# Chain and second inverse interleaved with latent attention, stick projections moved among the chunk preparations, chain products in 128 columns

## The chip, the cores and the metric

The kernel runs on one core of a Trainium2 chip. The metric is device time in microseconds from start to end of one execution. Five engines work side by side, each through its own queue in order: TensorE (PE; PEld is its weight load), VectorE (DVE), ScalarE (ACT), GpSimd (POOL) and SyncE (SP), which here issues every DMA.

## The reference

Two layers follow each other on a residual stream of 1024 positions by 1024 columns, float32. Each layer projects x to 2912 columns, which feed three kinds of heads, and mixes their results back:

```python
def stick_block(qb, start):          # 4 heads of 64, strict past only
    z = qb @ k.T * 64 ** -0.5
    log_keep = where(past, log_sigmoid(-z), 0)
    log_later = reverse_cumsum(log_keep) - log_keep
    return where(past, exp(log_sigmoid(z) + log_later), 0) @ v

def mla(q, k):                       # 4 heads: 64 plain + 32 rotary columns, causal
    return softmax(where(causal, q @ k.T * 96 ** -0.5, -inf)) @ v

def rwkv_step(state, r, w, k, v, kk, a):   # 8 heads, state 64 x 64, one step per position
    sa = state @ (-kk)
    state = state * w + sa * (kk * a) + v * k
    return state, state @ r

x = layer_norm(ALPHA * x + concat(o_sb, o_mla, o_rwkv) @ w_o)
u_act, u_gate = split(x @ ffn_w_up)
x = layer_norm(ALPHA * x + (gelu(causal_conv3(u_act)) * u_gate) @ ffn_w_down)
```

The per-position recurrence is computed in chunks of 64 positions: inside a chunk a triangular system has to be inverted, and between chunks a state is carried.

## The kernel before, in words

Every product that needs float32 accuracy splits its operands into a high and a low part and runs three matmuls (`mm3`, L200 to 204). A projection (`proj_h`, L241) computes 128 output columns for 1024 positions as 2 halves x 8 k-tiles x 3 = 48 matmuls of 512 columns. Its weights come through `wload` (L229): one DMA, a high part on ACT, a low part on DVE or POOL.

A layer runs in this order (`run`, L1117, and `phase_a`, L1046):

1. Projections and preparation of the latent heads (`mla_prep`).
2. Four chunk preparations, one per pair of recurrent heads: project k, r and v, then `rw_prep` and twice `rw_stage1` (L601; half the positions each), which make the chunk matrices and send them to DRAM. After the second and the fourth, `rw_inv` (L687) is made: a generator that inverts the triangles of four heads, mostly on DVE (L701 to 743), then on PE, and writes the result to DRAM. The first is stepped among the third and fourth preparation.
3. The gate's projection (`sg`), then the first chain (`rw_chain(0)`, L781) for heads 0 to 3, eight steps j of two chunks each, with the second inverse stepped three at a time between its steps.
4. The second chain, one step after each of the six stick projections (`proj_sb`, L260: two each of q, k and v; v is also transposed).
5. Attention: two streams of latent attention (`mla`, one per head of a pair) and two of stick attention (`stick`), 16 blocks of 128 queries each, in an order that `STREAM_ORDER` and `MLA_AHEAD` set.
6. Output projection, layer norm and feed-forward.

In a chain step, `rw_chain_q` (L799) loads four things from DRAM, multiplies them (L820) and brings the results to the tile QC (L821 to 823). `rw_chain_s` (L827) then does two state updates one after the other, each four products of 64 columns (L839) and two scalings on DVE (L842), and then the readout of eight products (L847). Such a float32 product is two instructions in the trace, so a step has 16 of them for its two updates and 16 for its readout. `rw_chain_y1` and `rw_chain_y2` normalise, add and gate.

A latent block takes scores on PE, a maximum on DVE (L541), an exponential on ACT (L546), a scaling on DVE (L559, L561), transposes (L327), and the product with v (L312). A stick block takes scores (L376, L377), a tanh on ACT (L378), a masking select on POOL (L384), and on DVE a scale (L385), a running product from the right (L387) and a combination (L388), then transposes and the product with v. A stick stream starts each head pair with copies and low-half splits of q and k (L350 to L361): on DVE for the first pair, on POOL in four pieces for the second.

The order on every engine is fixed when the program is built: a planner takes each engine's ready instructions by their place in the program, moved by the offsets in `PRIORITY` (weight loads and chain loads early, layer norms late). What a tile's buffers allow limits it. Of PSUM's eight banks, preparation and chains use pa 2, py 1, pq 1, mm 3, pi 1 (pi for the inverse); attention uses pa 2, py 1, pq 1, sc 2, av 2. The tag "pst" has four buffers that projections, attention loads and weights share.

Of the kernel before, what the change touches and what calls it, by code (L numbers as in the profile page):

```python
# [10 lines left out]
F32R = mybir.dt.float32r  # L11
# [30 lines left out]
MLA_AHEAD = 4  # L42
STREAM_ORDER = (-3, 0, 0, 1)
# [26 lines left out]
class Body:  # L70
# [38 lines left out]
    def constants(self):  # L109
# [23 lines left out]
        self.onesr = self.t(cp, [P, P], "onesr", F32R)  # L133
        nc.vector.tensor_copy(self.onesr, self.ones.to_broadcast([P, P]))
# [6 lines left out]
        self.m01 = self.t(cp, [P, W2], "m01")  # L141
        nc.vector.memset(self.m01, 1.0)
        nc.vector.memset(self.m01.rearrange("p (c i) -> p c i", i=C)[:, :, 0:1], 0.0)
# [116 lines left out]
    def proj_sb(self, l, pool, step):  # L260
        nc, W = self.nc, self.a["w_in"][l]
        for j in range(2):
            for base, dst in ((SBQ, self.sqd), (SBK, self.skd)):
                hi, lo = self.wload(W, [(base + j * P, P)], nc.gpsimd)
                d = self.t(pool, [P, S], "pst", bufs=4)
                self.proj_copy(hi, lo, d)
                nc.sync.dma_start(dst[j], d)
                step(4)
        for j in range(2):
            hi, lo = self.wload(W, [(SBV + j * P, P)], nc.gpsimd)  # L270
            d = self.t(pool, [P, S], "pst", bufs=4)
            self.proj_copy(hi, lo, d)
            o = self.t(pool, [P, S], "pst", bufs=4)
            for q in range(2):
                pt = self.ps2()
                for i in range(4):
                    ii = 4 * q + i
                    nc.tensor.transpose(pt[:, i * P : i * P + P], d[:, ii * P : ii * P + P], self.ident)
                nc.vector.tensor_copy(o[:, q * 512 : q * 512 + 512], pt)
            step(4)  # L280
            nc.sync.dma_start(self.svd[j], o.rearrange("p (i v) -> p i v", v=P))
# [38 lines left out]
    @prioritized  # L320
    def w_transpose(self, wt, w, nb, tag="av"):
# [59 lines left out]
    def stick_post(self, be, kp, i, LL, nb, n, V, hp, pr, wp):  # L381
        nc = self.nc
        dg = be[:, i * P : LL]
        nc.gpsimd.affine_select(out=dg, in_=dg, pattern=[[-1, P]], base=0, channel_multiplier=1, compare_op=ALU.is_gt, fill=-1.0)  # L384
        nc.vector.tensor_scalar(kp[:, : LL - 1], be[:, 1:LL], -0.5, 0.5, op0=ALU.mult, op1=ALU.add)  # L385
        kv = kp[:, : LL - 1][:, ::-1]
        nc.vector.tensor_tensor_scan(kv, kv, self.ones.to_broadcast([P, LL - 1]), 1.0, op0=ALU.mult, op1=ALU.mult)  # L387
        nc.vector.scalar_tensor_tensor(be[:, :LL], be[:, :LL], 1.0, kp[:, :LL], op0=ALU.add, op1=ALU.mult)  # L388
        wt = self.w_transpose(self.wt4[:, n % 6], be, nb, "pa")
        self.av_store(wt, nb, V, hp, self.mixd[pr], i, wp, "pa", 0.5)  # L390
# [20 lines left out]
    def mla_prep(self, l, mc, kp, wp):  # L411
        nc, a = self.nc, self.a
        ip = self.ip
        wr = self.t(kp, [P, 1280], "wr")
# [21 lines left out]
        def rms(js, n, gcol):  # L436
# [6 lines left out]
            for s in halves:  # L443
                ps = self.ps2()
                for j, (q, rows) in enumerate(sqs):
                    self.exact2(ps, self.onesr[:rows, :], q[:rows, s], wp, slice(0, rows))(j == 0, j == len(sqs) - 1)
                nc.scalar.activation(r[:, s], ps, AF.Ln, scale=1.0 / n, bias=self.rmse)
# [101 lines left out]
    def mla_post(self, st, e, pcs, n, nb, sc, pr, hp, i, V, wp):  # L549
# [12 lines left out]
        self.sn += 1  # L562
        wt = self.w_transpose(self.wt4[:, self.sn % 6], e, nb)
# [207 lines left out]
    def rw_chain_state(self, kp):  # L771
        nc = self.nc
        self.S_ = []
        for b in range(4):
            s_ = self.t(kp, [P, 2, 2, C], f"S{b}")
            nc.gpsimd.memset(s_, 0.0)
            nc.gpsimd.tensor_copy(s_[64:128, :, 0, :], self.ident[64:128, None, 64:128].to_broadcast([64, 2, 64]))
            nc.gpsimd.tensor_copy(s_[0:64, :, 1, :], self.ident[0:64, None, 0:64].to_broadcast([64, 2, 64]))
            self.S_.append(s_)

    def rw_chain(self, st, g2, tp):  # L781
        nc = self.nc
        for h in range(2):
            nc.gpsimd.memset(self.S_[0][h * 64 : h * 64 + 64, :, h, :], 0.0)
# [14 lines left out]
    def rw_chain_q(self, st, j, tp):  # L799
# [11 lines left out]
        QC = self.t(tp, [P, 2, 2, 2, P], "QC", bufs=2)  # L811
        PSh = PS.rearrange("p (f h) e x -> p f h e x", h=2)
        RBh = RB.rearrange("p (f h) c x -> p f h c x", h=2)
        for h in range(2):
            kr = slice(h * 64, h * 64 + 64)
            dr = slice(64 - h * 64, 128 - h * 64)
            pQ = self.pst("pa").rearrange("p (f e x) -> p f e x", f=2, e=2)
            for f in range(2):
                for e in range(2):
                    nc.tensor.matmul(pQ[:, f, e, :], PSh[:, f, h, e, :], RBh[:, f, h, e, :], start=True, stop=True)  # L820
# [6 lines left out]
    def rw_chain_s(self, st, j, QC):  # L827
        nc = self.nc
        fs = slice(2 * st, 2 * st + 2)
        ps = self.pst(("py", "pq")[j % 2])  # L830
        pY = ps[:, 0:256].rearrange("p (f h v) -> p f h v", f=2, h=2)
        pSS = ps[:, 256:512].rearrange("p (e f v) -> p e f v", e=2, f=2)
        for e in range(2):
            c_ = 2 * j + e
            Sc, Sn = self.S_[c_ % 4], self.S_[(c_ + 1) % 4]
            pS = pSS[:, e]
            for f in range(2):
                for h in range(2):
                    nc.tensor.matmul(pS[h * 64 : h * 64 + 64, f, :], QC[:, f, h, 1 - e, C:P], Sc[:, f, h, :], start=True, stop=True)  # L839
            for h in range(2):  # L840
                kr = slice(h * 64, h * 64 + 64)
                nc.vector.tensor_tensor(Sn[kr, :, h, :], pS[kr], self.Gc[kr, c_, fs, None].to_broadcast([64, 2, 64]), op=ALU.mult)  # L842
        for e in range(2):
            Sc = self.S_[(2 * j + e) % 4]
            for f in range(2):
                for h in range(2):
                    nc.tensor.matmul(pY[e * 64 : e * 64 + 64, f, h, :], QC[:, f, h, 1 - e, 0:C], Sc[:, f, h, :], start=True, stop=True)  # L847
        return pY

    def rw_chain_y1(self, pY, tp):  # L850
# [3 lines left out]
        py4 = pY.rearrange("p f h v -> p (f h) v")  # L854
        ys = self.t(tp, [P, 4, C], "ys", bufs=Y_LAG + 1)
        nc.scalar.copy(ys, py4)
# [189 lines left out]
    def phase_a(self, l, side, other, lp, co, cc):  # L1046
# [20 lines left out]
        self.split(*w2a2, raw)  # L1067
        self.Vz = []
# [12 lines left out]
        for ft in range(4):  # L1081
# [22 lines left out]
        ch = self.rw_chain(0, g2, tp)  # L1104
        for _ in ch:
            step(3)
        step(99)
        ch = self.rw_chain(1, g2, tp)

        def cstep(n):  # L1110
            next(ch, None)

        self.proj_sb(l, pp, cstep)
        for _ in ch:
            pass

    def run(self):  # L1117
# [28 lines left out]
        for l in range(L):  # L1146
# [6 lines left out]
            self.psum(cp, pa=(512, 2), py=(512, 1), pq=(512, 1))  # L1153
            with ExitStack() as c:
                self.psum(c, mm=(512, 3))
                self.psum(c, pi=(512, 1))
                cc = ExitStack()
                self.phase_a(l, side, other, lp, co, cc)
# [3 lines left out]
            with ExitStack() as c:  # L1162
                self.psum(c, sc=(512, 2), av=(512, 2))
                aw = self.pool(c, "attn", bufs=2, side=side)
                ms = [self.mla(aw, hp) for hp in range(2)]
                self.wt4 = self.t(self.ip, [P, 6, NT, P], "Aa")
                self.kp3 = [self.t(self.ip, [P, S], n) for n in ("LA", "T", "pd")]
                for t in self.kp3:
                    nc.gpsimd.memset(t, 0.0)
                for _ in range(MLA_AHEAD):  # L1170
                    next(ms[0])
                cc.close()
                self.w0h = self.t(self.wq, [P, 2, D], "w0h", F32R)
                self.w0l = self.t(self.wq, [P, 2, D], "w0l", F32R)
                aw3 = self.pool(c, "attn3", bufs=2, side=other)
                st = [self.stick(aw3, self.ip, hp) for hp in range(2)]
                seq = sorted([(t + o, n, g) for n, (g, o) in enumerate(zip((ms[0], st[0], ms[1], st[1]), STREAM_ORDER)) for t in range(17)], key=lambda x: x[:2])
                for _, _, g in seq:
                    next(g, None)
# [49 lines left out]
```

## Time and profile before

| what | value |
|---|---|
| time, median of 3 runs | 3151.99 us (3151.85 to 3153.93) |
| the profiled execution | 3154.05 us, span 3152.3 us |
| PE busy | 2993.2 us (95%) |
| DVE busy | 1796.4 us (57%) |
| ACT busy | 1058.6 us (34%) |
| POOL busy | 330.7 us (10%) |
| mean granted TensorE clock | 0.981 of full speed |

An engine is busy from an instruction's start to its end; matmuls are pipelined, so PE's busy time counts overlapping ones once and says little of how full it is. The chain that ended last is PE for 26% of the span, by 18% in three lines of `mm3`. A clock of 1.0 is 2.4 GHz, 0.5 is 1.2 GHz, and a mean in between is a mix of the two. Layer 1's mixer is at 128 to 746 us of the span, layer 2's at 1690 to 2305.

### The profile page before, as it was taken

What the parts mean: (1) busy time and instruction counts of PE and PEld (TensorE: products, weight loads), DVE (VectorE), ACT (ScalarE), POOL (GpSimd) and SP (SyncE); (2) the same over time, 40 slices, a digit from 0 to 9 for tenths busy, and PEclk for the clock granted to TensorE, in tenths of its full rate; (3) what the DMA queues carried; (4) which work ended last, traced back from release to release, by engine and by line L of the source; (5) the groups of instructions that cost most, each with busy time, mean ns of one, the idle gap of its engine ahead of it and who ended that gap; (6) DMA issues with size and microseconds to landing.
All of it is one profiled execution on the core that took longest, in us unless ns stands there. A gap on an engine that the chain in (4) does not pass through costs nothing. (4 is left out here: it accounts for less than half of the span.)

```text
span 3152.3 us, 42021 instructions
## 1 busy us (share of the span) xinstructions
PE 2993.2 (95%) x16572; PEld 2421.2 (77%) x16572; DVE 1796.4 (57%) x2842; ACT 1058.6 (34%) x1865; POOL 330.7 (10%) x346
## 2 busy tenths in 40 slices
PE   8998999988999999999999989999789999999998
PEld 6677777776888888888877767777678888888887
DVE  4587764876644444444746877567865444344436
ACT  5444343764122112222144443446532211122220
POOL 0112131132000000000001111311310000000000
PEclk9999899999999999999999999999899999999999
DMA  4344566323421111111234456662235111111111
GB/s 129 97 141 110 169 186 191 97 62 121 149 85 50 51 41 47 54 50 51 64 84 127 108 132 193 178 190 53 81 121 172 54 47 40 43 56 49 54 47 54
DMA packets 339284, 301.79 MB, mean 96 GB/s; under 512 B 25224, under 2 KB 304016, under 8 KB 339088
## 3 DMA queue, kind: packets, MB, share of 16 engines
q1 hardware_dynamic: 339088, 299.11, 32.1%
q8 instruction: 131, 2.15, 0.3%
q14 instruction: 65, 0.53, 0.1%
HBM read 208.87 MB, written 90.18 MB: 95 GB/s over the span
## 5 line engine op out<-in xcount | busy, mean ns | idle before, releaser
L202 PE MATMUL psmm<-xTh,whi 128*128 128x512 f32 x2144 | 852.9, 398 | 0.0
L204 PE MATMUL psmm<-xTh,wlo 128*128 128x512 f32 x2144 | 852.1, 397 | 0.0
L203 PE MATMUL psmm<-xTl,whi 128*128 128x512 f32 x2144 | 852.1, 397 | 0.0
L197 ACT CAST whi<-raw 128x1024 fp32r<-128x1024 f32 x152 | 159.9, 1052 | 1111.3 <-PE psmm L203 1076.1
L204 PEld LDWEIGHTS psmm<-xTh,wlo 128*128 128x128 f32 x2144 | 405.2, 189 | 93.2 <-issue 4.3
L202 PEld LDWEIGHTS psmm<-xTh,whi 128*128 128x128 f32 x2144 | 405.4, 189 | 92.9 <-issue 4.4
L203 PEld LDWEIGHTS psmm<-xTl,whi 128*128 128x128 f32 x2144 | 405.3, 189 | 92.8 <-issue 3.9
L198 DVE TENSOR_TENSOR wlo<-raw,whi 128x1024 fp32r<-128x1024 f32 x122 | 148.8, 1220 | 424.5 <-ACT whi L197 424.5
L1031 DVE TENSOR_TENSOR y<-y,psps 128x512 f32<-128x512 f32 x288 | 196.2, 686 | 171.8 <-PE psps L204 171.4
L202 PE MATMUL psps<-wdh,hh 128*128 128x512 f32 x672 | 266.8, 397 | 0.0
L203 PE MATMUL psps<-wdl,hh 128*128 128x512 f32 x672 | 263.1, 391 | 0.0
L204 PE MATMUL psps<-wdh,hl 128*128 128x512 f32 x672 | 260.1, 391 | 0.0
L894 POOL TENSOR_TENSOR lrs<-lrs,mhalf 128x1 f32<-128x1 f32 x32 | 29.1, 910 | 1637.7 <-DVE lrs L893 1637.7
L202 PEld LDWEIGHTS psps<-wdh,hh 128*128 128x128 f32 x672 | 126.1, 188 | 36.4 <-ACT hh L197 5.5
L204 PEld LDWEIGHTS psps<-wdh,hl 128*128 128x128 f32 x672 | 126.2, 188 | 27.0
L203 PEld LDWEIGHTS psps<-wdl,hh 128*128 128x128 f32 x672 | 126.3, 188 | 25.8
L1006 DVE TENSOR_TENSOR cv<-cv,psmm 128x1024 f32<-128x1024 f32 x44 | 53.7, 1221 | 143.3 <-PE psmm L204 138.4
L198 DVE TENSOR_TENSOR wdl<-raw,wdh 128x1024 fp32r<-128x1024 f32 x42 | 51.4, 1225 | 88.5 <-ACT wdh L197 88.5
L198 POOL TENSOR_TENSOR wlo<-raw,whi 128x1024 fp32r<-128x1024 f32 x30 | 76.0, 2532 | 242.5 <-ACT whi L197 242.4
L312 PE MATMUL pspa<-Aa,mv 128*128 128x128 f32 x576 | 86.4, 298 | 4.4 <-ACT Aa L328 3.8
L312 PEld LDWEIGHTS pspa<-Aa,mv 128*128 128x128 f32 x576 | 77.1, 207 | 17.5 <-ACT Aa L328 15.8
L820 PE MATMUL pspa<-RBl,PSl 128*128 128x128 f32 x512 | 73.4, 292 | 17.2 <-ACT QC L823 11.8
(443 smaller groups left out, 4777.4 us busy)
## 6 DMA issues: line engine op xcount, KB each, us to landing
raw<-in_ffn_w_up_dram SPq DMA_DIRECT2D x88, 512.0 KB
raw<-in_w_in_dram SPq DMA_DIRECT2D x44, 512.0 KB
raw<-in_ffn_w_down_dram SPq DMA_DIRECT2D x44, 512.0 KB
rbd<-RB SPq DMA_DIRECT2D x64, 256.0 KB
PSl<-psd SPq DMA_DIRECT2D x32, 512.0 KB
RBl<-rbd SPq DMA_DIRECT2D x32, 512.0 KB
psd<-Vz SPq DMA_DIRECT2D x64, 128.0 KB
xxd<-X SPq DMA_DIRECT2D x64, 128.0 KB
```

The costliest lines, as they stand in the source:

```text
L197: self.nc.scalar.copy(hi, src)
L198: (eng or self.nc.vector).tensor_tensor(lo, src, hi.bitcast(F32), op=ALU.subtract)
L202: mm(out, lh, rh, start=start, stop=False)
L203: mm(out, lh, rl, start=False, stop=False)
L204: mm(out, ll, rh, start=False, stop=stop)
L312: self.nc.tensor.matmul(av, V[:, j, :], wt[:, j, :], start=j == 0, stop=j == nb - 1)
L820: nc.tensor.matmul(pQ[:, f, e, :], PSh[:, f, h, e, :], RBh[:, f, h, e, :], start=True, stop=True)
L894: nc.gpsimd.tensor_tensor(rs, rs, self.mhalf[:, 0:1], op=ALU.pow)
L1006: nc.vector.tensor_tensor(cv, cv, pg, op=ALU.mult)
L1031: nc.vector.tensor_tensor(y[:, i, hs], y[:, i, hs], ps, op=ALU.add)
```

## The change

`proj_sb` becomes one projection per call and is called twice after each of the first three chunk preparations; the transposed v copies go from DVE to ACT. `phase_a` ends with the gate's projection and hands the second inverse and both chains, not yet run, to a new `phase_b`. There, for 19 turns, a chain step, three steps of the inverse, a block of the first latent stream and (three turns later) one of the second follow each other; the inverse is finished at turn 7, before the second chain begins, and the chains at turn 15. Stick attention follows alone, its two streams one turn apart. The bank pi stays through this, av has one buffer, and latent attention's transposes alternate between pi and av.

QC is laid out anew, so that one product takes both heads of a pair (for the states) or both chunks of a step (for the readout) in 128 columns; half of each result, the cross terms, is not used. `maskA`'s neighbours `onesr` and `m01` are made once a layer instead of once.

```diff
-    def proj_sb(self, l, pool, step):
+    def proj_sb(self, l, pool, n):
...
-                nc.vector.tensor_copy(o[:, q * 512 : q * 512 + 512], pt)
+            nc.scalar.copy(o[:, q * 512 : q * 512 + 512], pt)
...
-            pt = self.pst(tag)
+            pt = self.pst(tags[(j0 // 4 + 1) % len(tags)])
...
-        wt = self.w_transpose(self.wt4[:, self.sn % 6], e, nb)
+        wt = self.w_transpose(self.t(wp, [P, NT, P], "mwt", bufs=2), e, nb, ("av", "pi"))
...
-            nc.vector.tensor_tensor(QC[kr, :, h, :, 0:C], pQ[kr, :, :, 0:C], arl[kr], op=ALU.add)
-            nc.vector.tensor_tensor(QC[kr, :, h, :, C:P], pQ[kr, :, :, C:P], self.ident[kr, None, None, h * 64 : h * 64 + 64].to_broadcast([64, 2, 2, 64]), op=ALU.add)
-            nc.scalar.copy(QC[dr, :, h], pQ[dr])
+            nc.vector.tensor_tensor(QY[kr, :, h], pQ[kr, :, :, 0:C], arl[kr, :, ::-1, :], op=ALU.add)
+            nc.vector.tensor_tensor(QS[kr, :, :, h], pQ[kr, :, :, C:P], self.ident[kr, None, None, h * 64 : h * 64 + 64].to_broadcast([64, 2, 2, 64]), op=ALU.add)
+            nc.scalar.copy(QS[dr, :, :, h], pQ[dr, :, :, C:P])
+            nc.scalar.copy(QY[dr, :, h], pQ[dr, :, :, 0:C])
...
             for f in range(2):
-                for h in range(2):
-                    nc.tensor.matmul(pS[h * 64 : h * 64 + 64, f, :], QC[:, f, h, 1 - e, C:P], Sc[:, f, h, :], start=True, stop=True)
+                nc.tensor.matmul(pS[:, e, f], QC[:, 1, f, e], Sc[:, f], start=True, stop=True)
...
-                    nc.tensor.matmul(pY[e * 64 : e * 64 + 64, f, h, :], QC[:, f, h, 1 - e, 0:C], Sc[:, f, h, :], start=True, stop=True)
+                nc.tensor.matmul(pY[:, f, h], QC[:, 0, f, h], self.S_[j % 2][:, :, f, h, :], start=True, stop=True)
...
+            if ft < 3:
+                for n in range(2 * ft, 2 * ft + 2):
+                    self.proj_sb(l, pp, n)
...
+        return inv, [self.rw_chain(st, g2, tp) for st in range(2)]
+
+    def phase_b(self, l, side, other, c, cc, inv, chains):
+        nc = self.nc
+        aw = self.pool(c, "attn", bufs=2, side=side)
+        ms = [self.mla(aw, hp) for hp in range(2)]
+        for t in range(19):
+            if t < 16:
+                next(chains[t // 8], None)
+            if t == 15:
+                for ch in chains:
+                    for _ in ch:
+                        pass
+            for _ in range(3):
+                next(inv, None)
+            if t == 7:
+                for _ in inv:
+                    pass
+            if t < 16:
+                next(ms[0])
+            if t >= 3:
+                next(ms[1])
...
+        cc.close()
...
+        st = [self.stick(aw3, self.ip, hp) for hp in range(2)]
+        for t in range(18):
+            for n in range(2):
+                if t >= n:
+                    next(st[n], None)
```

## Rows read from the trace of the kernel before

**Rows 1.** The page, parts 1 and 2: busy time by engine, and by slice.
```profile
PE 2993.2 (95%) x16572; PEld 2421.2 (77%) x16572; DVE 1796.4 (57%) x2842; ACT 1058.6 (34%) x1865; POOL 330.7 (10%) x346
...
PE   8998999988999999999999989999789999999998
```
**Rows 2.** Busy time by stage: stretch, length, engines (instructions), clock, DMA share.
```profile
128.00:364.00 236.00, 213.94 (x1516) 169.06 (x1514) 173.25 (x296) 111.45 (x213) 49.29 (x50) 0.94 0.46 127
364.00:475.00 111.00, 101.92 (x946) 82.74 (x946) 81.56 (x156) 41.49 (x78) 29.23 (x24) 0.95 0.61 188
475.00:553.00 78.00, 74.18 (x559) 58.22 (x557) 34.65 (x94) 26.38 (x51) 14.70 (x15) 1.00 0.62 189
553.00:746.00 193.00, 169.83 (x1165) 145.78 (x1165) 153.10 (x309) 127.92 (x346) 44.17 (x55) 0.96 0.27 74
...
sum 615.00, PE 546.22 PEld 449.00 DVE 444.64 ACT 305.90 POOL 135.15; mean PE 136.56 PEld 112.25 DVE 111.16 ACT 76.48 POOL 33.79
```
**Rows 3.** PE's longest waits, 128 to 364 us: total, times, longest.
```profile
PE pspq L655 <- DVE q L632: 4.2, 1, 4.2
PE pspq L576 <- DVE q L198: 4.1, 1, 4.1
```
**Rows 4.** Stretches of the third preparation, columns as in rows 2.
```profile
223.00:238.00 15.00, 8.91 (x36) 6.41 (x34) 14.41 (x34) 6.47 (x11) 2.59 (x2) 0.87 0.14 37
...
257.00:270.00 13.00, 8.77 (x37) 7.12 (x37) 13.00 (x18) 4.69 (x11) 3.03 (x1) 0.80 0.16 42
```
**Rows 5.** PE in order of time, inside a projection: start, length.
```profile
180.32 0.39 PE L202 MATMUL psmm<-xTh,whi 128*128 128x512 f32 x1
180.55 0.40 PE L203 MATMUL psmm<-xTl,whi 128*128 128x512 f32 x1
```
**Rows 6.** DVE by line, 364 to 553 us: chain's and inverse's first and last.
```profile
L821 DVE TENSOR_TENSOR QC<-pspa,arl 64x256 f32<-64x256 f32 x32 | 13.5, 422 | 25.6 <-PE pspa L820 23.2 <-PE pspq L847 1.1 <-PE pspy L847 0.6
L705 DVE TENSOR_TENSOR pd<-LA,T 128x2 f32<-128x2 f32 (+18 forms) x19 | 13.5, 710 | 0.6
...
L859 DVE TENSOR_SCALAR vs<-vs 128x4 f32<-128x4 f32 x14 | 3.0, 213 | 0.2
...
L726 DVE STREAM_TRANSPOSE LA<-T 128x1024 f32<-128x1024 f32 x1 | 2.2, 2200 | 0.0
```
**Rows 7.** DVE by line, 553 to 746 us: latent's and sticks' first and last.
```profile
L541 DVE TENSOR_REDUCE mst<-pssc 128x1 f32<-128x512 f32 (+3 forms) x48 | 26.1, 548 | 7.6 <-PE pssc L204 5.4 <-PE pssc L539 2.1
L387 DVE TENSOR_TENSOR_SCAN pd<-pd,ones 128x255 f32<-128x255 f32 (+5 forms) x11 | 15.1, 1374 | 0.1
...
L361 DVE TENSOR_TENSOR kl<-pst,kh 96x1024 fp32r<-96x1024 f32 (+1 forms) x5 | 6.1, 1212 | 0.0
...
L385 DVE TENSOR_SCALAR T<-mexp 128x383 f32<-128x383 f32 (+5 forms) x11 | 5.0, 456 | 2.1 <-POOL mexp L384 2.0
...
L552 DVE RECIPROCAL mst<-mst 128x1 f32<-128x1 f32 x16 | 2.4, 153 | 4.2 <-ACT mexp L546 4.2
```
**Rows 8.** Stretches of chain with inverse, and of attention; columns as in rows 2.
```profile
364.00:440.00 76.00, 69.08 (x609) 55.15 (x608) 65.86 (x128) 26.83 (x49) 20.27 (x13) 0.96 0.64 201
...
553.00:640.00 87.00, 79.36 (x566) 67.72 (x567) 71.62 (x178) 63.52 (x182) 8.58 (x17) 1.00 0.32 86
```
**Rows 9.** POOL by line, 553 to 746 us: the sticks' splits.
```profile
L361 POOL TENSOR_TENSOR qh<-pst,qh 64x256 fp32r<-64x256 f32 x8 | 12.9, 1642 | 1.0 <-ACT qh L350 1.0
...
L361 POOL TENSOR_TENSOR kl<-pst,kh 128x256 fp32r<-128x256 f32 x8 | 8.6, 1098 | 4.6 <-ACT kh L351 4.6
```
**Rows 10.** PE in order of time, inside the first chain: start, length.
```profile
412.61 0.40 PE L847 MATMUL pspy<-S,QC 128*64 128x64 f32 x4
...
414.95 0.45 PE L839 MATMUL pspq<-S,QC 128*64 128x64 f32 x8
...
415.83 0.39 PE L876 MATMUL pspa<-sg,g 128*128 128x128 f32 x2
```
**Rows 11.** ACT by line, 364 to 553 us.
```profile
L823 ACT COPY QC<-pspa 64x512 f32<-64x512 f32 x32 | 18.6, 581 | 31.3 <-DVE QC L822 24.0 <-issue 6.0 <-PE pspa L820 0.9
```

More of the change, by code (lines that the diff above doesn't have):

```diff
@@ L258, in proj_T @@
         return pt
-    def proj_sb(self, l, pool, step):
+    def proj_sb(self, l, pool, n):
         nc, W = self.nc, self.a["w_in"][l]
[L262 to L278, printed above, removed]
-                nc.vector.tensor_copy(o[:, q * 512 : q * 512 + 512], pt)
-            step(4)
-            nc.sync.dma_start(self.svd[j], o.rearrange("p (i v) -> p i v", v=P))
+        j = n % 2
+        base, dst = ((SBQ, self.sqd), (SBK, self.skd), (SBV, self.svd))[n // 2]
+        hi, lo = self.wload(W, [(base + j * P, P)], nc.gpsimd)
+        d = self.t(pool, [P, S], "pst", bufs=4)
+        self.proj_copy(hi, lo, d)
+        if n < 4:
+            nc.sync.dma_start(dst[j], d)
+            return
+        o = self.t(pool, [P, S], "pst", bufs=4)
+        for q in range(2):
+            pt = self.ps2()
+            for i in range(4):
+                ii = 4 * q + i
+                nc.tensor.transpose(pt[:, i * P : i * P + P], d[:, ii * P : ii * P + P], self.ident)
+            nc.scalar.copy(o[:, q * 512 : q * 512 + 512], pt)
+        nc.sync.dma_start(dst[j], o.rearrange("p (i v) -> p i v", v=P))
     def proj_mla(self, l, pool):
@@ L413, in mla_prep @@
         ip = self.ip
+        onesr = self.t(kp, [P, P], "onesr", F32R)
+        nc.vector.tensor_copy(onesr, self.ones.to_broadcast([P, P]))
         wr = self.t(kp, [P, 1280], "wr")
@@ L445, in rms @@
                 for j, (q, rows) in enumerate(sqs):
-                    self.exact2(ps, self.onesr[:rows, :], q[:rows, s], wp, slice(0, rows))(j == 0, j == len(sqs) - 1)
+                    self.exact2(ps, onesr[:rows, :], q[:rows, s], wp, slice(0, rows))(j == 0, j == len(sqs) - 1)
                 nc.scalar.activation(r[:, s], ps, AF.Ln, scale=1.0 / n, bias=self.rmse)
@@ L853, in rw_chain_y1 @@
         vs = self.t(tp, [P, 4], "vs", bufs=Y_LAG + 1)
-        py4 = pY.rearrange("p f h v -> p (f h) v")
+        py4 = pY.rearrange("p f h e v -> p (f h) e v")
         ys = self.t(tp, [P, 4, C], "ys", bufs=Y_LAG + 1)
-        nc.scalar.copy(ys, py4)
+        for e in range(2):
+            er = slice(64 * e, 64 * e + 64)
+            nc.scalar.copy(ys[er], py4[er, :, e])
         nc.scalar.activation(yq, ys, AF.Square)
@@ L1067, in phase_a @@
         self.split(*w2a2, raw)
+        self.m01 = self.t(tp, [P, W2], "m01")
+        nc.gpsimd.memset(self.m01, 1.0)
+        nc.gpsimd.memset(self.m01.rearrange("p (c i) -> p c i", i=C)[:, :, 0:1], 0.0)
         self.Vz = []
@@ L1103, in phase_a @@
         self.rw_chain_state(kp)
[L1104 to L1115, printed above, removed]
+        return inv, [self.rw_chain(st, g2, tp) for st in range(2)]
[19 more added lines that the diff above has]
+                next(ms[1])
+        for m in ms:
+            next(m, None)
+        self.wt4 = self.t(self.ip, [P, 6, NT, P], "Aa")
+        self.kp3 = [self.t(self.ip, [P, S], n) for n in ("LA", "T", "pd")]
+        for t in self.kp3:
+            nc.gpsimd.memset(t, 0.0)
+        cc.close()
+        self.w0h = self.t(self.wq, [P, 2, D], "w0h", F32R)
+        self.w0l = self.t(self.wq, [P, 2, D], "w0l", F32R)
+        aw3 = self.pool(c, "attn3", bufs=2, side=other)
+        st = [self.stick(aw3, self.ip, hp) for hp in range(2)]
[3 more added lines that the diff above has]
+                    next(st[n], None)
     def run(self):
@@ L1152, in run @@
             self.Gc = self.t(lp, [P, NCH, 4], "Gc")
-            self.psum(cp, pa=(512, 2), py=(512, 1), pq=(512, 1))
+            self.psum(cp, pa=(512, 2), py=(512, 1), pq=(512, 1), pi=(512, 1))
             with ExitStack() as c:
                 self.psum(c, mm=(512, 3))
-                self.psum(c, pi=(512, 1))
                 cc = ExitStack()
-                self.phase_a(l, side, other, lp, co, cc)
+                inv, chains = self.phase_a(l, side, other, lp, co, cc)
             cx.close()
@@ L1162, in run @@
             with ExitStack() as c:
[L1163 to L1179, printed above, removed]
+                self.psum(c, sc=(512, 2), av=(512, 1))
+                self.phase_b(l, side, other, c, cc, inv, chains)
                 nxt = self.mix_load(NT - 1)
```

43 lines of the change are left out of this document (16 added, 27 removed).

## The prediction

> **What bounds the kernel now.** I read the page first: TensorE (PE) is busy 95% of the span, so at most about 159 us could come from filling its holes, and the slices place them: full in the feed-forward stretches, 7 to 9 tenths in the mixer stretches [rows 1]. Then the stage table, which cuts layer 1's mixer at 128, 364, 475, 553 and 746 us: chunk preparation, first chain with second inverse, second chain with stick projections, attention [rows 2]. The reader is to see there that no engine binds all four. In preparation VectorE (DVE) is busy 173 us and PE 214 of 236; in the first chain 82 and 102 of 111; in the second chain DVE only 35 of 78, because six projections keep PE full; in attention 153 and 170 of 193. Layer 2's four stretches sum to 615 us against 618. A busy PE is not a full PE: back-to-back 512-column matmuls start every 0.23 us but each is drawn 0.39 us long [rows 5], so PE's figures are upper ends and DVE's can be summed. Third, who waits in preparation: PE waits for DVE, 4.2 and 4.1 us at the longest [rows 3], in two stretches where DVE is busy 96 to 100%, PE only 59 to 67%, and the granted clock falls to 0.87 and 0.80 of 2.4 GHz [rows 4]. The last view is the DVE groups by line, from which each stream's load is summed.
>
> **The change, part by part, for one layer.**
>
> *Projections into preparation.* Six projections of 48 matmuls leave the second chain: 288 x 0.23 = 66 us of PE [rows 5]; the same 66 us go into preparation. DVE gets nothing with them (the weights' low halves are split on POOL, busy 49 of 236 us there [rows 2]); the two transposed V copies move from DVE to ACT. What can come back is PE's waste in the 236 us: 236 - 213.9 = 22 us not busy, and a mean clock of 0.94, which means 12% of the time at 1.2 GHz, a loss of at most 0.06 x 236 = 14 us. So the refund lies between 0 and 36 us. I take half, 18 us: the two projections after the second preparation give the first inverse's DVE work 22 us more to run under, and that is where both long waits and the low clock stand [rows 3, 4]. The other half stays, since the short waits of PE on masks and squares happened although projections were already there as filler. Each projection needs one of four "pst" buffers, of which k, r and v hold three, so no more than about one runs ahead inside a preparation. Preparation: 236 + 66 - 18 = 284 us, so +48.
>
> *Chains, second inverse and latent attention together, sticks alone.* Before, 364 to 746 us is 382 us; without the 66 us of projections 316. After, DVE binds. Its load by stream: the chains' eight groups run from 13.5 down to 3.0 us and sum to 66.0, with 4.0 more after 553: 70 us. The inverse's seven groups, 13.5 to 2.2, sum to 48 us [rows 6]. Latent attention's eight groups, 26.1 to 2.4, sum to 64, and eight low-half splits of 1.21 us make 74. The sticks' nine scan, scale and product groups, 15.1 to 5.0, sum to 86, and their four splits make 91 [rows 7]. First pass (chains, inverse, latent attention) 70 + 48 + 74 = 192 us, second pass (sticks) 91 us; with sg's shift, 284. PE and ACT have slack: ACT was busy 41 + 26 + 128 = 196 of these 382 us [rows 2]. DVE's share of such a stretch is the whole question: 0.82 where four attention streams run (553 to 640), 0.87 where chain and inverse run with projections (364 to 440) [rows 8], 0.96 to 1.00 where inverse and preparation saturate it [rows 4]. I take 0.88, near the second, since the first pass keeps the inverse's DVE-only ladder as filler for its first half: 284 / 0.88 = 322 us, +6 against 316. Of it the sticks take about 106 (91 plus some 15 for the small blocks and the change of head pair). The ends: 0.96 gives 296 (-20), attention's whole 153.1/193 = 0.79 gives 359 (+43).
>
> *Products in 128 columns.* Eight state-product instructions of 64 columns take 0.45 us with the last 0.22 us long, so seven starts in 0.23 us: two at a time. The readouts come singly, four in 0.40 us, 0.06 apart; a 128-column fp32 piece starts 0.11 after the one before [rows 10]. A chain step had 16 + 16 such pieces, 16/2 x 0.058 + 16 x 0.058 = 1.39 us, and gets 8 + 8 of 0.112 = 1.79: +0.4 x 16 steps = 6 to 7 us of PE. If every state round waits for its products it is also 32 x 0.22 = 7 us of path; I charge 0, since DVE and not PE binds the first pass, and keep 7 as the upper end.
> The Trainium skill, TensorE: Matmul & The Clock Gate, Part 3, says that matmuls with few output rows run at the same time when their outputs lie in different column groups. By that rule all 32 pieces would have gone in pairs, and the loss would be 0.86 x 16 = 14 us a layer; the rows show pairs for the state products alone, so 7 is the bound I keep.
>
> *Copies and single buffers.* QC leaves PSUM in 64 ACT copies of 256 elements instead of 32 of 512, which took 0.58 us [rows 11]; if each costs 0.29 (half) to 0.58 it is 0 to +19 us of ACT, under ACT's slack of half the stretch. A readout copy becomes two. Latent attention's transposes lose one PSUM buffer: behind a waiting transpose stand all of PE's later matmuls, and a copy of 0.58 exposed in each of 32 blocks would be 19 us; I charge 0 while DVE is behind, 19 at most. All DMAs go through SP's queue: the chains' 64 loads now stand among the attention's stores, and a store that waits for its block holds the next chunk's load; two chunks are in flight at some 14 us each, so 0, and if that cover fails one load's wait per chunk is in the 0.79 end. Memsets of m01 and onesr, once a layer: under 1 us, hidden.
>
> *Sum.* Per layer +48 for preparation, -66 + 6 = -60 for the rest: -12. Two layers: -24. The profiled execution took 3154.05 us (span 3152.3), 2.1 above the median 3151.99: 3130 in its terms, 3128 in the median's.
>
> **Rivals.**
>
> *The stick pass starves* (slower). Place: the 32 stick blocks. Today latent attention's reductions fill DVE while a stick block goes PE, ACT, POOL select, DVE; one of the sticks' three scale groups still idled 2.1 us for that select [rows 7]. Alone, two streams must cover it, and at the change of head pair POOL splits q and k for 12.9 + 8.6 = 22 us [rows 9], of which the two widest blocks in hand cover about 10 (86 us over 32 blocks is 2.7 us at a mean width of 576, so 4.8 at 1024). At a DVE share of 0.70 the pass is 91/0.70 + 12 = 142 instead of 106: +36 over the forecast, per layer -12 + 36 = +24, in all 3128 + 72 = 3200. It decides from a stick pass of about 118 us. Against it: three blocks are in flight, and two widest ones hold DVE for 9.6 us.
> The Trainium skill, Perfetto Trace Analysis, Optimization Strategy, advises interleaving regimes whose most contended engine differs. The second chain did that, with DVE busy 35 and PE 74 of 78 us [rows 2]; the change pairs DVE-heavy with DVE-heavy. It speaks for this side, by no figure of its own.
>
> *Everything fills* (faster by more). The whole 36 us comes back and DVE runs at 0.93 (305 us, -11): -47 a layer, 3058. For: DVE already reaches 0.96 and more where it has enough ready [rows 4]. Against: neither of the longer stretches reached 0.9 [rows 8].
>
> *No change.* The planner already used projections as filler, so moved ones only displace others: refund 6, rest +6, 3152.
>
> **How the numbers follow.** Forecast 0.38, stick starvation 0.32, everything fills 0.15, no change 0.15. About 0.2% (6 us) is what a measurement of this kernel can tell from no change. The forecast's own spread is a DVE share of 0.86 to 0.91 (330 to 312) with the refund fixed: 3108 to 3144. Faster: 0.34 + 0.15 + 0.03 = 0.52; same: 0.03 + 0.09 = 0.12; slower: 0.32 + 0.01 + 0.03 = 0.36. The range goes down to 3065, which leaves out half of "everything fills", and up to 3210, which leaves out about a third of the starvation cases: together a little under 2 in 10.
>
> **What would show it.** Preparation from the first mask multiply to the last should take about 284 us a layer, with PE's waits on DVE during the first inverse gone and the clock there at 1.0; if it takes 300, the refund failed. From there to the output projection some 322 us, DVE at 0.88 or above; the stick scans (L387 before) should lie in their own stretch of about 106 us, and a stretch of 118 or more with DVE waiting for POOL's select and splits is the rival. The chain products should be half as many, 0.11 us apart, and no wait of DVE on them should grow past 7 us a layer. Wrong altogether if layer 1's mixer is longer than 618 us.

## The result, and the profile after

The changed kernel took 3285.77 us (median of 4 runs, 3275.36 to 3290.04) beside 3152.96 us of the kernel before: 1.0416 times as long, interval 1.0389 to 1.0442, so 133 us slower. The forecast was 3128 us, in a range of 3065 to 3210. The profiled execution took 3288.49 us, span 3286.8.

The page after, parts 1 and 2, answering to [rows 1]:

```profile
PE 3050.8 (93%) x16060; PEld 2470.1 (75%) x16060; DVE 1794.7 (55%) x2833; ACT 1081.9 (33%) x1969; POOL 343.3 (10%) x346
...
PE   8998988967999999999999989789679999999998
```

DVE's work is the same to 2 us, and the feed-forward slices are as full as before. What is new are emptier slices in the two mixers. The stage table says where (stretch, length, busy time of PE, PEld, DVE, ACT and POOL with their instructions, granted clock, DMA share, GB/s); layer 1 in five stretches (preparation; first chain with the inverse; the joint between the chains; second chain; sticks alone), layer 2's three below (preparation; chains with latent attention; sticks), and last the preparation of layer 2 in the kernel before:

```profile
128.00:437.00 309.00, 284.80 (x1817) 219.20 (x1815) 178.85 (x296) 126.22 (x234) 56.82 (x53) 0.97 0.40 114
437.00:540.00 103.00, 76.41 (x632) 67.44 (x628) 90.22 (x200) 46.36 (x122) 17.45 (x13) 0.82 0.60 182
540.00:590.00 50.00, 43.13 (x333) 37.63 (x333) 23.48 (x64) 28.12 (x72) 5.45 (x7) 0.86 0.50 128
590.00:684.00 94.00, 82.61 (x619) 74.03 (x617) 61.27 (x191) 58.29 (x174) 15.59 (x18) 0.96 0.39 120
684.00:808.00 124.00, 88.51 (x518) 73.83 (x518) 99.28 (x106) 65.45 (x141) 51.74 (x52) 0.82 0.29 85
sum 680.00, PE 575.45 PEld 472.13 DVE 453.10 ACT 324.44 POOL 147.06; mean PE 115.09 PEld 94.43 DVE 90.62 ACT 64.89 POOL 29.41
...
1752.00:2067.00 315.00, 290.63 (x1843) 225.68 (x1843) 180.31 (x299) 128.93 (x237) 58.69 (x56) 0.96 0.43 116
2067.00:2316.00 249.00, 202.63 (x1581) 179.78 (x1581) 174.82 (x454) 132.96 (x367) 38.37 (x38) 0.89 0.49 147
2316.00:2440.00 124.00, 87.82 (x518) 72.64 (x518) 100.20 (x107) 65.46 (x141) 52.53 (x52) 0.82 0.30 86
...
1690.00:1921.00 231.00, 207.33 (x1499) 164.63 (x1498) 173.10 (x294) 109.82 (x211) 46.03 (x50) 0.95 0.48 128
```

Layer 1's mixer is 680 us instead of 618, layer 2's 688 (315 + 249 + 124) instead of 615 [rows 2]: +62 and +73, together 135, the whole loss. Preparation grew by 73 us in layer 1 and 84 in layer 2, where +48 was forecast. From there to the output projection 371 us stand against 382 (373 against 384 in layer 2), where 322 were forecast. So the 66 us of projections cost more than their length where they went, and all the rest gave back 11.

### The profile page after: what moved, and what is told of

It is laid out like the page before. It is cut to its first block, busy times and chain, and to the rows that moved or that the text cites. A ratio compares the mean times of both kernels' runs of the same rounds, so it can differ in the third digit from the quotient of the medians.

```text
span 3286.8 us, 41212 instructions
## 1 busy us (share of the span) xinstructions
PE 3050.8 (93%) x16060; PEld 2470.1 (75%) x16060; DVE 1794.7 (55%) x2833; ACT 1081.9 (33%) x1969; POOL 343.3 (10%) x346
## 5 line engine op out<-in xcount | busy, mean ns | idle before, releaser
L195 PE MATMUL psmm<-xTh,whi 128*128 128x512 f32 x2144 | 852.1, 398 | 0.0
L197 PE MATMUL psmm<-xTh,wlo 128*128 128x512 f32 x2144 | 850.4, 397 | 0.0
L195 PEld LDWEIGHTS psmm<-xTh,whi 128*128 128x128 f32 x2144 | 404.6, 189 | 96.8 <-issue 7.5
L197 PEld LDWEIGHTS psmm<-xTh,wlo 128*128 128x128 f32 x2144 | 404.7, 189 | 96.0 <-issue 7.8
L195 PE MATMUL psps<-wdh,hh 128*128 128x512 f32 x672 | 266.8, 397 | 0.0
L197 PE MATMUL psps<-wdh,hl 128*128 128x512 f32 x672 | 260.1, 391 | 0.0
L195 PEld LDWEIGHTS psps<-wdh,hh 128*128 128x128 f32 x672 | 126.1, 188 | 36.5 <-ACT hh L190 5.5
L197 PEld LDWEIGHTS psps<-wdh,hl 128*128 128x128 f32 x672 | 126.2, 188 | 27.0
L301 PE MATMUL pspa<-Aa,mv 128*128 128x128 f32 x576 | 93.6, 313 | 19.6 <-ACT Aa L317 19.4
L301 PE MATMUL psav<-mwt,mv 128*128 128x128 f32 x576 | 86.6, 295 | 9.0 <-ACT mwt L317 3.8
```

What stands on the lines that cost most here:

```text
L195: mm(out, lh, rh, start=start, stop=False)
L197: mm(out, ll, rh, start=False, stop=stop)
L301: self.nc.tensor.matmul(av, V[:, j, :], wt[:, j, :], start=j == 0, stop=j == nb - 1)
```

## The experiments

Each time below stands beside runs of the kernel before on the same chip; the interval is the ratio's. The kernels are named by what they edit.

**The chain products alone.** The kernel before with only the changed chain functions (new QC, products of 128 columns, two ACT copies).

```diff
-                    nc.tensor.matmul(pS[h * 64 : h * 64 + 64, f, :], QC[:, f, h, 1 - e, C:P], Sc[:, f, h, :], start=True, stop=True)
+                nc.tensor.matmul(pS[:, e, f], QC[:, 1, f, e], Sc[:, f], start=True, stop=True)
...
```

> The kernel before with nothing but the 128-column chain products (QC's layout, S, readout and its two copies). Theory A (the time is lost to the order of the work: DVE starves at two joints that the new order makes): no change, 3147 to 3160. Theory B (it is lost to the new products, copies and banks): slower by the 7 us a layer of extra TensorE work and up to 19 us of ACT copies, 3167 to 3205.

Measured: 3162.0 us against 3151.91, 1.003 [1.002, 1.004]. That is between the two theories' ranges. The new products with their copies and banks cost 10 us, 5 a layer, inside the bound of 7 that the prediction kept. Charging nothing was wrong by that much.

**The sticks last, alone.** The kernel before with its streams so ordered that sticks begin when latent attention is nearly done.

```diff
-STREAM_ORDER = (-3, 0, 0, 1)
+STREAM_ORDER = (-3, 17, 0, 18)
```

> The kernel before with one constant changed, so that the stick streams come after all latent blocks instead of among them; banks, buffers and projections stay. Theory A: the sticks then need their own 110 to 125 us and the latent blocks, without chain work beside them, 85 to 100 where both took 193 together: +10 to +30 a layer, 3172 to 3212. Theory B: no change, 3147 to 3160.

Measured: 3167.56 against 3151.91, 1.0051 [1.0037, 1.0066]: +16 us, 8 a layer, between the two theories' ranges. The rival of the starving sticks has a real price, but in this kernel it is no more than an eighth of the loss.

**The projections alone.** The kernel before with the six stick projections among the preparations, as in the change; chains, inverse and attention stay in their old order, the second chain without projections beside it.

```diff
+            if ft < 3:
+                for n in range(2 * ft, 2 * ft + 2):
+                    self.proj_sb(l, pp, n)
...
-        self.proj_sb(l, pp, cstep)
```

> The kernel before with the six stick projections moved among the chunk preparations and the second chain left without them; attention, products and banks stay. Preparation should then take 300 to 310 us as in the changed kernel (it took 236), and the second chain, 78 us with projections, falls to what its own latency gives. Theory A: the chain alone is bound by its round trips at 40 to 50 us, so a layer gains nothing and loses 35 to 45: 3222 to 3245. Theory B (the chain was held only by the projections beside it): 12 to 20 us, no loss, 3150 to 3175.

Measured: 3286.11 against 3151.91, 1.0431 [1.0415, 1.0446]: +134 us, above both theories. This one part costs as much as the whole change. Its stages in layer 1 (preparation; both chains; attention):

```profile
128.00:437.00 309.00, 284.52 (x1833) 218.34 (x1832) 181.47 (x299) 127.08 (x237) 56.97 (x55) 0.98 0.41 117
437.00:630.00 193.00, 148.89 (x1371) 127.84 (x1370) 130.92 (x310) 79.11 (x176) 36.82 (x38) 0.77 0.57 171
630.00:812.00 182.00, 148.31 (x984) 127.61 (x983) 135.12 (x244) 110.32 (x285) 42.82 (x52) 0.91 0.23 63
```

Without any projection the chains need 193 us; with all six they took 111 + 78 = 189 [rows 2].

**Are projections beside the chains free?** Two kernels test this. The first is the kernel before with each stick projection cut to one of its eight k-tiles (so q, k and v of the sticks are left incomplete, and 58 of the 66 us of PE are gone from a layer). The second does the six projections twice, in the preparations and beside the second chain.

```diff
-                self.proj_copy(hi, lo, d)
+                self.proj_copy(hi, lo, d, 1)
```

> The kernel before with 7 of the 8 k-tiles of the six stick projections left out (42 of their 48 matmuls each; their loads, splits, copies and stores stay): 2 x 252 x 0.23 = 116 us less TensorE work beside the chains. Theory A (beside the chains the projections are free: the stretch from 364 to 553 us is set by the second inverse and then by the second chain's own pace): no change, 3140 to 3165. Theory B (the prediction's step: they hold the chains up by their own 66 us a layer): 3035 to 3060.

Measured: 3168.82 against 3151.69, 1.0054 [1.0039, 1.0069]. With 116 us of matmuls less, the kernel is 17 us slower, 4 us above theory A's range and over 100 above theory B's.

> The kernel before with the six stick projections computed twice, once among the chunk preparations and once more beside the second chain, the same values stored again: 132 us of TensorE work more than either kernel, over both layers. Theory A (among the preparations they cost their whole length, beside the chains nothing, and there they keep the granted clock up): 3270 to 3300, no slower than with the move alone (3286). Theory B (a projection costs its matmuls wherever it stands): 3390 to 3425.

Measured: 3305.03 against 3152.52, 1.0486 [1.0468, 1.0503]. A second set, 132 us of matmuls, costs 19 us over the kernel with the projections in the preparations alone; 5 us above theory A's range and 85 under theory B's. Its preparation and its attention, against 236 and 193 us before [rows 2]:

```profile
128.00:438.00 310.00, 284.60 (x1829) 218.40 (x1827) 181.73 (x298) 127.50 (x235) 59.18 (x56) 0.97 0.41 118
...
628.00:817.00 189.00, 165.67 (x1133) 143.13 (x1131) 151.95 (x301) 126.28 (x341) 43.97 (x55) 0.95 0.27 74
```

The first set stands in the preparation and makes it 74 us longer; behind it next to nothing grew.

The stretch of both chains, one row for each: the kernel before, the shortened projections, the doubled ones.

```profile
364.00:553.00 189.00, 176.10 (x1503) 140.96 (x1502) 116.21 (x250) 67.87 (x129) 43.93 (x38) 0.97 0.62 188
```
```profile
364.00:553.00 189.00, 128.59 (x1245) 109.64 (x1244) 116.42 (x249) 66.17 (x129) 46.25 (x39) 0.79 0.60 185
```
```profile
438.00:628.00 190.00, 176.96 (x1513) 141.76 (x1511) 116.62 (x254) 68.01 (x130) 44.82 (x39) 0.97 0.61 187
```

PE's busy time goes from 129 to 177 us and the stretch stays at 189 to 193. What moves with it is the granted clock, 0.79 and 0.77 without the projections, 0.97 with them.

The unchanged length is a balance of two effects, and both can be read in the traces. First the end of the second inverse, from its last transposes on VectorE to its last product, then the second chain, from its first product to its last readout; of each the kernel before and the shortened projections:

```profile
449.00:478.00 29.00, 27.93 (x310) 24.09 (x311) 7.31 (x21) 13.86 (x27) 8.83 (x10) 0.94 0.59 164
451.00:486.00 35.00, 21.54 (x226) 19.39 (x226) 5.52 (x15) 9.16 (x18) 5.75 (x8) 0.65 0.43 113
...
487.00:555.00 68.00, 64.18 (x523) 50.38 (x523) 36.01 (x100) 23.90 (x48) 10.79 (x12) 1.00 0.59 186
494.00:553.00 59.00, 45.94 (x439) 39.71 (x440) 35.12 (x95) 22.27 (x47) 10.77 (x12) 0.90 0.57 186
```

Without the projections the inverse's end takes 6 us longer: PE is busy 22 of 35 us instead of 28 of 29, the clock is 0.65 instead of 0.94, and the median of the last 64 products goes from 275 to 421 ns. The second chain then takes 9 us less. (In layer 2, from the same events: 32 us instead of 26, and 59 instead of 64.) So the projections do slow the chain, and they keep up the clock under which the inverse before it ends; here the two nearly cancel.

In layer 1 the loss lies behind the chains: attention runs at a clock of 0.92 instead of 0.96, and the work after it comes 12 us later than before; why was not settled.

**What sets the chains' length?** First the inverse, stepped sooner beside the first chain of the kernel before.

```diff
         for _ in ch:
-            step(3)
+            step(6)
```

> The kernel before with the second inverse stepped six times instead of three after each step of the first chain. Theory A (the stretch from the last preparation to the attention is one line: inverse's VectorE work, its matmul tail, second chain; the first chain ends some 35 us before the second can start, so its turn can be given to the inverse): the inverse's VectorE part, 85 us, ends 5 to 20 us sooner and the second chain starts as much sooner: 3112 to 3142. Theory B (that line is not the bound): 3147 to 3157.

Measured: 3161.46 against 3153.73, 1.0026 [1.0015, 1.0037].

> The same with twelve steps, so that the inverse is ahead of nearly all of the first chain. Theory A: its VectorE part ends 15 to 30 us sooner, but the first chain, pushed back, then ends after the inverse and holds the second chain itself (both use one set of states): 3100 to 3150. Theory B: 3147 to 3157.

Measured, with 12: 3165.1, 1.0042 [1.0029, 1.0055]. Both are slower, and outside both theories' ranges, so the theory that the inverse alone holds the chains fell. The second chain's first product came 4 and 12 us sooner than before (483.0 and 475.2 us instead of 487.2), its last readout 5 us later (559.5 instead of 554.1). With the projections in place they are a second line of about the same length. So both were eased at once: 12 steps and the shortened projections (the same part of the computation left out).

> The kernel before with both things that moved little alone: 7 of 8 k-tiles of the stick projections left out (alone 3169) and the second inverse stepped twelve times (alone 3165). Theory A (two lines of about equal length run through the chain stretch, the inverse with the second chain and the interleaved projections with it; taking one away leaves the other): together they shorten it by 10 to 20 us a layer, 3120 to 3145. Theory B (neither is the bound; the chains' own steps are): 3155 to 3180.

Measured: 3149.79 against 3152.52, 0.9992 [0.9982, 1.0002], between what the two theories gave it. Against the shortened kernel it is 19 us faster, and the second chain's last readout comes at 541.6 us instead of 552.6. Against the kernel with 12 steps and whole projections it is some 14 us faster: there the projections were not free. The inverse counts once the projections are gone, and two lines side by side are the picture that fits all four; that nothing else holds the chain is not shown.

**Projections in the preparations, shortened.** The changed kernel with the same cut.

```diff
-        self.proj_copy(hi, lo, d)
+        self.proj_copy(hi, lo, d, 1)
```

> The changed kernel with the same matmuls left out, now among the chunk preparations. Theory A (there TensorE is on the path, so they cost their whole length): 3286 - 116 = 3170, within 3160 to 3195. Theory B (preparation is held by VectorE and hides at least half of them): 3225 to 3290.

Measured: 3213.16 against 3151.69, 1.0189 [1.0169, 1.021], between the two forecasts and in neither. Its preparation:

```profile
128.00:408.00 280.00, 245.00 (x1579) 185.58 (x1578) 182.64 (x298) 124.94 (x236) 58.97 (x53) 0.89 0.45 128
```

Here leaving out 116 us of matmuls gives 73 back; where they stood before it gave back none. But 280 us are still 44 more than 236, with 8 us of those matmuls left: the six calls also displace other work, by an amount that is measured and whose parts are not.

**The joint between the chains.** In the changed kernel, the inverse stepped nine at a time and ended at turn 3.

```diff
-            for _ in range(3):
+            for _ in range(9):
                 next(inv, None)
-            if t == 7:
+            if t == 3:
```

> The changed kernel with the second inverse stepped nine times a turn and finished at turn 3 instead of three times and turn 7, nothing else. Theory A: the second chain no longer waits for the inverse's matmul tail (540 to 590 us, where DVE was busy 23.5 of 50), so 10 to 25 us a layer come back: 3235 to 3265. Theory B: the order of the inverse does not matter, 3275 to 3295.

Measured: 3278.44 against 3151.91, 1.0411 [1.0388, 1.0434], in theory B's range: 7 us under the changed kernel, with intervals that overlap. The inverse's last product ends at 544.7 us instead of 574.9 and the second chain begins at 556.5 instead of 584.6, yet its last readout ends at 664.8 instead of 667.6. A start 28 us sooner is worth 3: the second chain beside latent blocks is held by something else.

**The bank pi.** In the changed kernel, latent attention's transposes keep to av.

```diff
-        wt = self.w_transpose(self.t(wp, [P, NT, P], "mwt", bufs=2), e, nb, ("av", "pi"))
+        wt = self.w_transpose(self.t(wp, [P, NT, P], "mwt", bufs=2), e, nb, ("av",))
```

> The changed kernel with latent attention's transposes in the av bank alone, so that pi serves the inverse alone. Theory A (the inverse's tail and the second chain set the first pass; pi is a small part of it): the tail from its last transposes to its last product, 533 to 575 us, shrinks by up to 10 us, but av becomes the only bank for latent attention: 3270 to 3300. Theory B (sharing pi is what holds the inverse): 3230 to 3260.

Measured: 3248.92 against 3151.69, 1.0318 [1.0293, 1.0344], in theory B's range and 37 us under the changed kernel. Users of pi in the changed kernel's layer 1 (durations least, median, most; first and last start):

```profile
L316 PE MATMUL pspi<-ident,mexp x40: 271/274/473, 458.7 to 579.1; 128*128 128x128 f32 x40
L754 PE MATMUL pspi<-LA,Aa x32: 274/421/582, 537.1 to 559.3; 128*128 128x128 f32 x32
...
L754 PE MATMUL pspi<-T,Aa x32: 273/275/377, 547.2 to 574.6; 128*128 128x128 f32 x32
```

and without the transposes in it:

```profile
L754 PE MATMUL pspi<-LA,Aa x32: 275/275/521, 537.2 to 556.1; 128*128 128x128 f32 x32
...
L754 PE MATMUL pspi<-T,Aa x32: 275/275/377, 542.3 to 559.9; 128*128 128x128 f32 x32
```

The inverse's last products go through the one bank of this tag. With 40 transposes in the same bank they end 15 us later, and the second chain waits for them. Two buffers for the transposes were worse than one. That the gain comes by the inverse alone is not shown: in the run before, an inverse that ended 30 us sooner gained 3 at the chain's end, and the edit here also keeps the latent blocks' transposes from waiting for the inverse's products. The first 32 of these products ran at a lower clock besides (0.80 against 0.94), with a median of 421 ns against 275 without the transposes.

**A better place for the projections?** In the kernel before, the six projections beside the first chain and the inverse, and the second chain stepped among the first latent blocks.

```diff
+        def cstep(n):
+            next(ch, None)
+            step(4)
+
+        self.proj_sb(l, pp, cstep)
         for _ in ch:
             step(3)
         step(99)
-        ch = self.rw_chain(1, g2, tp)
...
+        self.ch1 = self.rw_chain(1, g2, tp)
...
-                for _ in range(MLA_AHEAD):
+                for t in range(8):
+                    next(self.ch1, None)
                     next(ms[0])
+                    if t >= 3:
+                        next(ms[1])
```

> A version that could beat both: the kernel before, but with the six stick projections beside the first chain and second inverse, and the second chain beside the first blocks of latent attention; sticks then join latent attention as before. Theory A (chain stretches have TensorE time to spare: 87 of 111 us and VectorE 82): the first stretch grows from 111 to 125 to 135 us, and second chain with all attention takes 235 to 255 where it took 78 + 193: 3115 to 3165. Theory B (VectorE is the bound everywhere, so joining chain and attention gives nothing): 3165 to 3200.

Measured: 3188.91 against 3151.69, 1.0117 [1.0102, 1.0132]. Slower by 37, in theory B's range, yet 97 under the changed kernel: second chain and latent attention merged, with the projections kept beside a chain. No version with the whole computation beat the kernel before.

## Why the prediction was wrong, step by step

**The step that failed first** is the credit of -66 in the sum's "-66 + 6 = -60 for the rest", by the sentence "Before, 364 to 746 us is 382 us; without the 66 us of projections 316." It takes a stage's length for the sum of what its engines do. The prediction itself had seen that "no engine binds all four" and that PE is full in the second chain "because six projections keep PE full", a filling and no bound. In the arithmetic the 316 cancels: the 322 after is DVE's 284 us over a share of 0.88, so the -60 hangs on "After, DVE binds", and that is where it broke. The runs show in its place: without the projections the chains took 193 us instead of 189, with a second set of them 190, and in the changed kernel DVE was busy 274 of 371 us, a share of 0.74. The rest fell by 11 us a layer and not by 60, which is 98 us of the miss; the preparation, +73 and +84 instead of +48, is 61. Together they are, to 2 us, the 157 between the forecast -24 and the measured +133.

**Preparation: 284 forecast, 309 measured; the refund of 18 came out as -7** (-18 in layer 2: 231 + 66 forecast without a refund, 315 measured). The prediction's own sign for that, "if it takes 300, the refund failed", holds. The two waits of [rows 3] went, but PE's idle time did not: 24 us of 309, against 22 of 236 before. A short wait became the longest. The row of the kernel before, then the same line's in the changed kernel:

```profile
PE pspq L575 <- ACT q L197: 1.9, 1, 1.9
...
PE pspq L565 <- ACT q L190: 16.7, 3, 13.2
```

The engine named, ACT, was itself waiting. ACT in order of time, with what it waited for, and then DVE in the microseconds before:

```profile
289.46 1.15 ACT L581 ACTIVATE kk<-pst,pv 128x1024 f32<-128x1024 f32 x1 [14.38 <-DVE pst L296]
```
```profile
280.40 0.74 DVE L296 SCALAR_TENSOR_TENSOR pst<-psmm,pv,pst 128x511 f32<-128x511 f32 x1
281.06 1.44 DVE L695 TENSOR_TENSOR pd<-T,M 128x768 f32<-128x768 f32 x1
282.53 0.95 DVE L696 TENSOR_REDUCE T<-pd 128x64 f32<-128x768 f32 x1
283.51 1.88 DVE L695 TENSOR_TENSOR pd<-T,M 128x1024 f32<-128x1024 f32 x1
285.43 1.22 DVE L696 TENSOR_REDUCE T<-pd 128x64 f32<-128x1024 f32 x1
286.69 2.02 DVE L716 STREAM_TRANSPOSE LA<-T 128x1024 f32<-128x1024 f32 x1
288.55 0.17 DVE L293 TENSOR_TENSOR pst<-pst,shc 128x1 f32<-128x1 f32 x1
288.58 0.79 DVE L296 SCALAR_TENSOR_TENSOR pst<-psmm,pv,pst 128x511 f32<-128x511 f32 x1
```

DVE has done the first half of a projection's shift (L296 at 280.40); the second half stands behind five inverse instructions, 7.5 us. PE meanwhile, by the stage table's columns and in order of time:

```profile
275.00:293.00 18.00, 4.72 (x17) 3.00 (x15) 17.55 (x22) 2.90 (x5) 0.20 (x1) 0.67 0.11 30
```

```profile
277.68 0.39 PE L195 MATMUL psmm<-xTh,whi 128*128 128x512 f32 x1
291.31 0.80 PE L565 MATMUL pspq<-q,bonesr 128*128 128x512 f32 x1 [13.25 <-ACT q L190]
291.90 0.63 PE L196 MATMUL psmm<-xTl,whi 128*128 128x512 f32 x1
```

PE is busy 5 of 18 us, at a clock of 0.67. A projection is broken off here: L195 to L197 are the three matmuls of one `mm3`, and between its first, at 277.68, and its second, at 291.90, PE's queue holds the product that waits. So filler was at hand and stood behind the wait. More filler in a stretch is none in the place where PE waits; the prediction gave it to "the first inverse's DVE work" without asking where in the queues it would stand.

**"After, DVE binds", at a share of 0.88.** In the first 103 us, while the inverse's DVE ladder runs, DVE is busy 90.2/103 = 0.88, as forecast. In the 144 us after it the share is 0.59 (84.8 us). Over the first pass DVE had 175 us of work, near the forecast's 192, in 247 us: share 0.71, not 0.88, +48 against 175/0.88 = 199 (and +31 against the 216 that the forecast leaves beside the sticks' 106). The named cover ("the inverse's DVE-only ladder as filler for its first half") was right and its end was not priced. The delay in the joint is partly the shared pi bank above; what paces the second chain after it stays open.

**The sticks' pass: 106 forecast, 124 measured**, and in the second layer 124 too: past the 118 from which the rival decides. Its sign, DVE waiting for POOL, is there (DVE's waits for POOL by total, times and longest, 684 to 808 us), and so are the splits of [rows 9]:

```profile
DVE LA L374 <- POOL mexp L373: 4.8, 2, 3.2
DVE T L374 <- POOL mexp L373: 4.6, 5, 3.9
DVE pd L374 <- POOL mexp L373: 3.7, 3, 2.2
```
```profile
L350 POOL TENSOR_TENSOR qh<-pst,qh 64x256 fp32r<-64x256 f32 x8 | 13.5, 1709 | 1.2 <-issue 1.0
L350 POOL TENSOR_TENSOR kl<-pst,kh 128x256 fp32r<-128x256 f32 x8 | 9.9, 1257 | 3.5 <-ACT kh L340 3.5
```

So this rival was right in place and half right in size: +18 a layer here, not +36. But its mechanism is only part of that. DVE had 99 us of work where 91 were forecast, and was idle 25 where 15 were; of the 25, 13 are these waits for POOL, and the kernel before had 10 of them already, two of the three scale groups waiting longer than the one that [rows 7] shows:

```profile
L385 DVE TENSOR_SCALAR pd<-mexp 128x255 f32<-128x255 f32 (+5 forms) x11 | 5.5, 498 | 3.2 <-POOL mexp L384 3.2
L385 DVE TENSOR_SCALAR LA<-mexp 128x511 f32<-128x511 f32 (+2 forms) x10 | 5.1, 514 | 5.1 <-POOL mexp L384 5.0
```

Even with the rival whole the time would have been 3200.

**Small terms.** The products in 128 columns start 0.11 us apart, half as many, as forecast: four in 0.61 us, the last of them drawn long.

```profile
642.00 0.61 PE L827 MATMUL pspy<-S,QC 128*128 128x128 f32 x4
```

DVE's waits on the state products stayed under the 7 us that the prediction set as a sign (437 to 684 us: total, times, longest):

```profile
DVE S L830 <- PE pspy L827: 4.0, 6, 1.4
```

By themselves, with their copies, they cost 5 us a layer, where 0 was charged and 7 kept as the end. The 14 us that the prediction worked out beside the 7 rest on a misreading of the kernel before: its readouts go four after another to the same 64 output rows (e is the outer loop, L844 to 847), and only the state products alternate between two sets of rows, so pairs for these alone, as [rows 10] has them, are what the rule cited there gives. The copies of QC (the two lines, then those of [rows 11] against them) are 23.5 us of ACT instead of 18.6, +5 of 0 to 19:

```profile
L816 ACT COPY QC<-pspa 64x256 f32<-64x256 f32 x32 | 11.8, 368 | 0.0
L815 ACT COPY QC<-pspa 64x256 f32<-64x256 f32 x32 | 11.7, 366 | 23.9 <-DVE QC L814 21.7 <-PE pspa L812 1.2 <-PE psav L301 0.8
```

The transposes' buffer was charged 0, at most 19 a layer for the one lost; the cost lay in the one that they gained, 37 us over both layers.

**The merge.** With the projections moved, merging chains and latent attention brought nothing more or less (3286.11 without, 3285.77 with). The costs that runs put a figure to are 37 (pi), 16 (sticks last, in the kernel before) and 10 (128 columns); if they add up, the merge itself gained some 63 us and spent it again. That they add was not tested.

The Trainium skill, Perfetto Trace Analysis, Optimization Strategy, says that regimes with different most-contended engines can gain from being interleaved. The kernel before had done so: a chain that leaves DVE idle for more than half of its time (35 of 78 us busy [rows 2]), beside projections that fill PE. Taking that pair apart cost 134 us (3286.11 against 3151.91), so the runs agree. The prediction named this pair, but counted it for the starving sticks and gave its loss no price.

## What to carry to other kernels

Before a moved piece of work is subtracted from the stretch it leaves, ask what the stretch's length is made of: where a sequence of dependent steps sets it, the filler beside it costs little and gives little back, and in a stretch that is already full it is paid for. The test is cheap: cut the filler to an eighth where it stands and see whether the time moves, and look at the granted clock too, since a stretch that keeps its length may hide a gain and a loss. And filler helps only at the place in the queues where an engine would wait, and a shared single PSUM bank can tie two streams together that the order meant to be apart.

## What the hardware showed that was not expected

Taking TensorE work out of a stretch lowered its granted clock, from 0.97 to 0.79 over the 189 us of the chains, and the kernel became 17 us slower with 116 us of matmuls less. The stretch kept its length at either clock, but not because the clock cost nothing: at 0.65 instead of 0.94, mostly 1.2 instead of mostly 2.4 GHz, the end of the second inverse took 35 us instead of 29, and the chain behind it, with less beside it, took 59 instead of 68.
